# A two-layer hybrid attention block on one core: the later modulation sums move to VectorE, and the first projections are cut in two around three gate blocks

## The chip, the cores and the metric

The kernel runs on one core of a Trainium2 chip. The metric is device time in microseconds (us), the median of several runs of one launch. All inputs and outputs are fp32 in device memory. The engines that matter here are TensorE (PE, matmuls and transposes), VectorE (DVE), ScalarE (ACT), GpSimd (POOL) and the sync engine (SP), from whose queue nearly all transfers are issued. Each engine runs its own instructions in the order in which they were written down.

## The reference, cut to what matters

Two layers over 512 latent tokens and 256 context tokens of width 2048. In each layer a conditioning vector is multiplied by a matrix of 2048 x 6144 and gives shift, scale and gate; this is the modulation. The normalised input times scale plus shift goes through one input projection that feeds three groups of attention heads (A: neighbourhood, B: sliding window, C: latent attention with compressed q and kv) and a gate path z; the heads' outputs times silu(z) go through an output projection, and the result times gate is added to the input.

```
for l in range(DEPTH):                      # DEPTH = 2
    shift, scale, gate       = split(silu(c)     @ w_ada[l] + b_ada[l], 3)
    shift_c, scale_c, gate_c = split(silu(c_ctx) @ w_ada[l] + b_ada[l], 3)
    h  = rms(x,  norm_w[l]) * (1 + scale)   + shift      # 512 latent tokens
    hc = rms(xc, norm_w[l]) * (1 + scale_c) + shift_c    # 256 context tokens
    u  = h @ w_in[l]          # q, k, v of A and B; compressed q and kv, key of C; z
    y  = concat(o_a, o_b, o_c) * silu(z)
    x  = x + gate * (y @ w_out[l])
    # layer 0 does the same for xc; layer 1 needs only k and v of the context
```

There are two vectors, c for the latent tokens and c_ctx for the context, so each modulation block has two sides. In layer 1 only the latent side of the gate is used.

## The kernel before, in words

**Layout.** Tokens are six tiles of 128 (four latent, two context). The modulated input is held transposed, as 16 k-tiles of 128 features by 768 tokens, each split into a high and a low part (hT), and every weight is split likewise ("wh" and "wl", lines 234 and 228 by the helpers sub and act): a product is the sum of three reduced-precision matmuls, high by high, high by low and low by high. A TJob (line 419) is a projection whose output has tokens on the partitions: for each piece of two k-tiles it issues 36 matmuls of 256 columns over three banks of accumulators. An FJob (line 514) makes a block of 128 gate features: four pieces of four k-tiles, in two banks of 384 tokens each. A Group (line 492) takes the pieces of several jobs in turn.

**Planner.** The program is written by a planner, class Weaver: strands of work (fibers) with priorities run against a virtual clock, with a cost for each instruction (lines 210 to 290) and for each transfer (start, line 289: a queue step of 0.475 us, then bytes at 3.6e5 a microsecond). A strand may issue an instruction only when its engine's planned backlog is below AHEAD = 1.35 us. So the order on every engine, SP's queue among them, follows from planned times and priorities; on the chip only semaphores decide when an instruction starts. The list of jobs (main) has priority 6, the lowest; two attention workers and the weight splitter have 2, what comes behind a projection has 1.

**Buffers.** 52 buffers "s3" of 128x768 hold x, hT, heads, and the first modulation weights; "wa" has four buffers of 128x512 for the later ones; "ws" three for weights as loaded. PSUM has six banks "g" and a pair "S", which serves the attention scores and, in the first projections, two of q's banks.

**Modulation.** ada_blocks (line 687) goes through blocks of columns of w_ada. A load is 256 KB, 128 rows by 512 columns (or two k-tiles by 256). Up to depth loads are ahead; a group of them is then multiplied on PE at line 722, with the conditioning vector as 32 columns of weights and the loaded tile streaming through. The four k-tiles of a group stand in different rows of 32 of one bank. ada_finish (line 731) copies the bank, and at line 739 a matmul against the constant "sel" transposes it and adds the four rows. The bias is added, and events tell make_hk that a k-tile's shift and scale are there.

**Order.** Layer 0's shift and scale run at the start in blocks of 256 columns, alternating, with ten loads ahead in groups of two; each pair of blocks releases two k-tiles of hT. The first job is a Group of kv and q of the first two heads of A, piece by piece, as k-tiles are released. Then gate block 0, then the other heads of A and B with gate blocks 1 to 9 among them. Layer 0's gate is started as a strand of priority 4 behind B. Then come C's compressed projections, the rotary key (kpe) and gate blocks 10 to 15, which are stored to device memory; after them hT is freed. Then C's heads, with layer 1's shift and scale beside them in layer 0, and layer 1's gate in layer 1. Last is the output projection, whose last rounds (post_out) multiply by the gate.

post_chunk (line 869) is what follows a kv or q job: per bank, ScalarE copies it out ("raw"), squares and sums follow, then norms, rotary, transposes and the split into heads.

## Time and profile before

| | |
|---|---|
| median of 3 runs | 2972.59 us (2969.92 to 2973.67) |
| the profiled execution | 2976.81 us, of which the span of instructions is 2975.0 |
| granted TensorE clock, mean | 0.994 |
| bytes moved | 349.23 MB, 117 GB/s over the span |
| the first 32 us | PE busy 1.27, the DMA engines full (share 1.02) |
| 32 to 57 us | PE busy 23.00 of 25.00, DMA share 1.02 |
| matmuls on "wa" | from 922.6 to 2692.5 us |

How to read it: a busy share is of the whole span, and one average covers stages with different limits. Busy time of PE counts overlapping matmuls once but holds their pipeline's tail, so that a full row need not mean a full stream. PEld is the loading of PE's weights, which overlaps the matmuls. fp32 matmuls leave two records each in the trace, so that one modulation matmul counts twice. A line such as L234 is that of a helper, and the tile names beside it tell which step it serves. Windows give busy time per engine in the order PE, PEld, DVE, ACT, POOL, then the granted clock, the mean share of the 16 DMA engines, and GB/s.

### The profile page before, as it was taken

The page shows a single profiled execution, that of the slowest core. Times are in us where ns is not written, and L with a number is a line of the kernel's source. Part 1 is how long each engine was busy: PE and PEld are TensorE (multiplying, and loading weights), DVE is VectorE, ACT ScalarE, POOL GpSimd, SP SyncE. Part 2 cuts the span into 40 slices and gives each one's busy share as a digit, 9 for nine tenths or more (in the row PEclk, how much of TensorE's full clock was granted, in tenths as well). Part 3 has the DMA queues.
Part 4 walks back from the last instruction along what each step waited for, and adds up shares of the span by engine and source line. Part 5 has one row for each costly group of instructions (what it writes and reads, how often), then busy time and mean ns, then how long its engine had stood idle before and what let it go on. Part 6 is the DMA issues. An engine that isn't in the chain of part 4 may idle for free.

```text
span 2975.0 us, 56930 instructions
## 1 busy us (share of the span) xinstructions
PE 2882.8 (97%) x21819; PEld 2706.2 (91%) x21819; DVE 1758.5 (59%) x4820; ACT 1254.2 (42%) x2730; POOL 140.1 (5%) x189
## 2 busy tenths in 40 slices
PE   5999999999999999999999999999999999999998
PEld 3689999999999899878999989999998999788998
DVE  5345554637757473867634374655677676578643
ACT  4234333425545452545422273443445455346421
POOL 3000000000100010000000000000000000000000
PEclk9999999999999999999999999999999999999999
DMA  9842222221224555547334333333322214543244
GB/s 253 281 136 81 72 78 76 65 70 49 63 60 127 171 145 157 193 150 237 111 111 124 111 104 82 93 96 91 86 73 66 77 59 129 178 156 118 87 154 127
DMA packets 423633, 349.23 MB, mean 117 GB/s; under 512 B 66276, under 2 KB 370210, under 8 KB 423360
## 3 DMA queue, kind: packets, MB, share of 16 engines
q1 hardware_dynamic: 421488, 344.27, 38.7%
q0 software_dynamic: 1872, 1.32, 0.4%
q8 instruction: 171, 2.80, 0.4%
q14 instruction: 102, 0.84, 0.1%
HBM read 303.97 MB, written 32.08 MB: 113 GB/s over the span
## 4 chain that ended last, share of the span: by engine, by line
PE 88%; DVE 5%; DMA 4%; SPq 1%; ACT 1%; issue 1%; DVEq 0%; ACTq 0%
PE g L323 71%; PE S L323 7%; PE g L326 6%; PE g L722 3%; SPq L293 1%; DMA s<-w_ada 1%; DMA s<-scr 1%; ACT s L228 1%; DVE wl L234 1%; DVE s L234 1%; DVE s L267 1%; DVE pt L234 1%; PE g L739 1%; DVE tm L234 0%; DVE s L256 0%
## 5 line engine op out<-in xcount | busy, mean ns | idle before, releaser
L323 PE MATMUL g<-wh,s 128*128 128x256 f32 (+1 forms) x9000 | 1761.5, 289 | 17.1 <-DVE s L234 7.5
L323 PEld LDWEIGHTS g<-wh,s 128*128 128x128 f32 x9000 | 1445.8, 192 | 54.2 <-issue 31.5
L323 PE MATMUL g<-wl,s 128*128 128x256 f32 (+1 forms) x4500 | 1284.5, 285 | 3.0 <-DVE wl L234 3.0
L323 PEld LDWEIGHTS g<-wl,s 128*128 128x128 f32 x4500 | 862.9, 192 | 5.3 <-DVE wl L234 3.9
L234 DVE TENSOR_TENSOR wl<-ws,wh 128x512 fp32r<-128x512 f32 (+1 forms) x598 | 409.7, 686 | 566.2 <-PE g L323 445.9
L228 ACT ACTIVATE wh<-ws 128x512 fp32r<-128x512 f32 (+2 forms) x606 | 372.0, 615 | 471.8 <-PE g L323 428.2
L323 PE MATMUL g<-s,wh 128*128 128x384 f32 (+1 forms) x1664 | 465.2, 356 | 0.9 <-ACT tm L228 0.9
L228 ACT ACTIVATE s<-s,sm 128x640 f32<-128x640 f32 (+3 forms) x260 | 195.8, 753 | 379.9 <-DVE sm L267 295.4
L323 PEld LDWEIGHTS g<-s,wh 128*128 128x128 f32 x1664 | 304.4, 188 | 21.1 <-ACT tm L228 1.1
L323 PE MATMUL g<-s,wl 128*128 128x384 f32 (+1 forms) x768 | 271.7, 354 | 0.0
L228 ACT ACTIVATE tm<-g 128x512 f32<-128x512 f32 (+4 forms) x324 | 160.7, 517 | 247.6 <-PE g L323 147.5
L234 DVE TENSOR_TENSOR pt<-g,pt 128x512 fp32r<-128x512 f32 (+1 forms) x338 | 196.4, 591 | 92.3 <-ACT pt L228 91.1
L323 PE MATMUL S<-s,s 128*128 128x256 f32 (+2 forms) x1260 | 238.8, 318 | 6.5 <-DVE sm L267 6.1
L326 PE MATMUL g<-ident,s 128*128 128x128 f32 x1520 | 232.7, 277 | 9.8 <-DVE s L234 6.1
L228 ACT ACTIVATE pt<-g 128x512 fp32r<-128x512 f32 (+1 forms) x338 | 168.7, 516 | 155.6 <-PE g L326 149.9
L323 PE MATMUL g<-pt,s 128*128 128x256 f32 (+1 forms) x1348 | 216.7, 286 | 7.4 <-DVE pt L234 4.8
L323 PEld LDWEIGHTS S<-s,s 128*128 128x128 f32 x1260 | 187.2, 190 | 28.6 <-DVE sm L267 12.1
L326 PEld LDWEIGHTS g<-ident,s 128*128 128x128 f32 x1520 | 177.3, 142 | 36.1 <-issue 12.6
L323 PEld LDWEIGHTS g<-pt,s 128*128 128x128 f32 x1348 | 186.5, 192 | 17.6 <-DVE pt L234 7.2
L277 POOL TENSOR_TENSOR s<-ot,s 64x256 f32<-64x256 f32 x100 | 79.3, 794 | 1922.2 <-DVE ot L234 1905.9
L323 PEld LDWEIGHTS g<-s,wl 128*128 128x128 f32 x768 | 144.7, 188 | 9.7 <-DVE wl L234 0.2
L251 DVE TENSOR_SCALAR s<-s,sm 128x640 f32<-128x640 f32 (+3 forms) x260 | 131.8, 507 | 6.1
(146 smaller groups left out, 2129.9 us busy)
## 6 DMA issues: line engine op xcount, KB each, us to landing
wa<-w_ada SPq DMA_DIRECT2D x256, 256.0 KB
ws<-w_in SPq DMA_DIRECT2D x328, 128.0 KB
ws<-w_in SPq DMA_DIRECT2D x160, 256.0 KB
ws<-w_out SPq DMA_DIRECT2D x136, 256.0 KB
s<-w_ada SPq DMA_DIRECT2D x128, 256.0 KB
s<-scr SPq DMA_DIRECT2D x36, 384.0 KB
ws<-w_in SPq DMA_DIRECT2D x64, 192.0 KB
ws<-w_qb SPq DMA_DIRECT2D x54, 192.0 KB
```

The costliest lines, as they stand in the source:

```text
L228: self.nc.scalar.activation(out, in_, func, bias=bias, scale=scale, **kw)
L234: self.nc.vector.tensor_tensor(out, a, b, op=op)
L251: self.nc.vector.tensor_scalar(out, a, s1, s2, op0=op0, op1=op1)
L267: self.nc.vector.tensor_tensor_reduce(out, a, b, -1.0, init, OP.add, OP.min, acc)
L277: self.nc.gpsimd.tensor_tensor(out, a, b, op=OP.mult)
L293: self.nc.sync.dma_start(out, in_)
L323: self.nc.tensor.matmul(out, l, r, start=start, stop=stop, skip_group_check=True)
L326: self.nc.tensor.transpose(out, in_, self.ident)
L722: nc.tensor.matmul(ps[j:j + 32, :n], scT[:, kk, :], s[:, x * n:(x + 1) * n], start=kk < 4, stop=kk >= 12, skip_group_check=True)
L739: nc.tensor.matmul(pt[:, 2 * c:2 * c + 2], a[:, c * 128:(c + 1) * 128], sel, start=c == 0, stop=c == m - 1, skip_group_check=True)
```

## The change

It has four parts.

1. **Later modulation on VectorE.** Layer 0's gate and all of layer 1's modulation no longer pass through PE at line 722. A strand ada_rest, of priority 5, starts once layer 0's shift and scale are done and goes through gate 0, shift and scale 1, gate 1. For each block of 512 columns and each k-tile, VectorE multiplies the loaded tile by the conditioning vector's 128 values for that k-tile (a scalar for each partition) and adds it to an accumulator "ac", one for each side; the strand then pauses for PACE = 4.0 us of planned time. At the block's end, PE adds up the 128 partitions with matmuls of each 128 columns against a column of ones. "wa" and "ac" have two buffers each in place of four "wa". Layer 1's gate is made for the latent side alone.
2. **First projections in two halves.** kv and q of the first two heads become two jobs each, of eight k-tiles. The first halves' banks are copied to "s3" by ScalarE (keep_part); three gate blocks, 10, 11 and 12, follow as a Group, one of them in "S"; then the second halves, to which VectorE adds the copies.
3. **First bursts.** Layer 0's shift and scale run with twelve loads ahead in groups of four (ten and two before).
4. **Planner's costs.** A transfer is planned at 3.1e5 bytes a microsecond, and the matmuls behind a modulation block at 0.21 us (0.05 before).

```diff
-RES = dict(wa=0, s3=8)
+HALF = 8
+RES = dict(s3=8)
+PACE = 4.0
...
-        w.clk["dma"] = max(w.clk["dma"], q + 0.65) + b / 3.6e5
+        w.clk["dma"] = max(w.clk["dma"], q + 0.65) + b / 3.1e5
...
+    def ada_vec(l, c0s, sides):
+        n = 512
+        items = [(c0, k) for c0 in c0s for k in range(KT)]
+        pend = deque()
+        nxt = 0
+        for c0 in c0s:
+            acc = []
+            for k in range(KT):
+                while nxt < len(items) and (not pend or K.free("wa")):
+                    w.cur.ft = w.vt
+                    s = yield from K.get("wa")
+                    c_, k_ = items[nxt]
+                    nxt += 1
+                    ts = yield from K.load_ahead(s, t["w_ada"][l, k_ * 128:(k_ + 1) * 128, c_:c_ + n])
+                    pend.append((s, ts))
+                s, ts = pend.popleft()
+                yield from K.wait(ev_c)
+                w.cur.ft = max(w.vt, ts)
+                if k == 0:
+                    for _ in sides:
+                        acc.append((yield from K.get("ac")))
+                for a, m in zip(acc, sides):
+                    sc = scT[:, k, m:m + 1]
+                    if k == 0:
+                        yield from K.ts(a, s, sc, OP.mult, fast=True)
+                    else:
+                        yield from K.stt(a, s, sc, a, OP.mult, OP.add)
+                K.put("wa", s)
+                yield w.vt + PACE
+            pt = yield from K.get("g")
+            yield from K.sync()
+            for c in range(n // 128):
+                for a, m in zip(acc, sides):
+                    nc.tensor.matmul(pt[:, 2 * c + m:2 * c + m + 1], a[:, c * 128:(c + 1) * 128], one,
+                                     start=c == 0 and m == sides[0], stop=c == n // 128 - 1 and m == sides[-1],
+                                     skip_group_check=True)
+            w.pe(0.21 * n // 128 * len(sides))
+            K.put("ac", *acc)
+            w.spawn(ada_use(l, c0, n, pt, sides), 1, w.cur.ft)
...
+                if part is not None:
+                    yield from K.wait(part[b][1])
+                    yield from K.add(raw, ps[b], part[b][0][:, :512])
+                    K.put("s3", part[b][0])
+                    K.put("g", ps[b])
+                    pv = rv
+                elif direct:
...
+        def keep_part(part):
+            def gen(ps, done):
+                for b in range(len(ps)):
+                    yield from K.wait(done[b])
+                    part[b][0] = yield from K.get("s3")
+                    yield from K.act(part[b][0][:, :512], ps[b])
+                    K.put("g", ps[b])
+                    K.set(part[b][1])
+            return gen
...
+            return [TJob(K, W, runs, cut, tiles, lhs_h, ev_h, keep_part(part)),
+                    TJob(K, W, runs, KT - cut, tiles, lhs_h, ev_h, post, room_chunk(G, blocks), k0=cut)]
...
+            if cut:
+                zs = [zjob(f) for f in (10, 11, 12)]
+                q[0].inS = zs[2].inS = True
+                jobs.extend([Group([kv[0], q[0]]), Group(zs), Group([kv[1], q[1]]), zjob(p)])
...
-        if l == 0:
-            J(lambda: w.spawn(ada_gate(0, "wa", "g", 4, 4), 4))
...
-        for f in range(10, KT):
+        for f in range(10 if last else 13, KT):
...
-        J(lambda: w.spawn(ada_scale(1, 512, "wa", "g", 4, 4) if l == 0 else ada_gate(1, "wa", "g", 4, 4), 4))
...
-    w.spawn(ada_scale(0, 256, "s3", "g", 10, 2), 3)
+    def modulation():
+        yield from ada_scale(0, 256, "s3", "g", 12, 4)
+        w.spawn(ada_rest(), 5)
+
+    def ada_rest():
+        yield from ada_gate(0)
+        yield from ada_vec(1, [c + o for c in range(0, D, 512) for o in (0, D)], (0, 1))
+        yield from ada_gate(1)
+
+    w.spawn(modulation(), 3)
```

More of the change, by code (lines that the diff above doesn't have):

```diff
@@ L544, in step @@
             if p == 0:
-                self.ps[i] = yield from K.get("g")
+                if self.inS:
+                    if i == 0:
+                        pair = yield from K.halves()
+                    self.ps[i] = pair[i]
+                else:
+                    self.ps[i] = yield from K.get("g")
             K.w.cur.ft = tp
@@ L747, in ada_finish @@
         K.put("g", pt)
-        K.put("tm", a)
         k0 = f % KT
@@ L762, in ada_scale, with ada_gate @@
         yield from ada_blocks(l, [(c + o, n) for c in range(0, D, n) for o in (0, D)], stag, ptag, depth, group)
-    def ada_gate(l, stag, ptag, depth, group):
-        yield from ada_blocks(l, [(2 * D + c, 512) for c in range(0, D, 512)], stag, ptag, depth, group)
+    def ada_gate(l):
+        sides = (0, 1) if l == 0 else (0,)
+        yield from ada_vec(l, [2 * D + c for c in range(0, D, 512)], sides)
         yield from K.wait(*ev_gb[l])
@@ L768, in ada_gate @@
         yield from K.sync()
-        for m in range(2):
+        for m in sides:
             K.tr(ps[:KT, m * 128:(m + 1) * 128], ada[l][:, 32:48, m])
@@ L1412, in chunk @@
                     runs.append((c0, 64))
+            part = None if cut is None else [[None, Event()] for _ in range(0, len(tiles), 2)]
             def post(ps, done):
```

56 lines of the change are left out of this document (33 added, 23 removed).

## The prediction

> **What bounds the kernel now.** I read the page's busy times and the chain that ended last, then the table of stretches, then single stretches by line and by time.
>
> ```profile
> span 2975.0 us, 56930 instructions
> PE 2882.8 (97%) x21819; PEld 2706.2 (91%) x21819; DVE 1758.5 (59%) x4820; ACT 1254.2 (42%) x2730; POOL 140.1 (5%) x189
> PE 88%; DVE 5%; DMA 4%; SPq 1%; ACT 1%; issue 1%; DVEq 0%; ACTq 0%
> PE g L323 71%; PE S L323 7%; PE g L326 6%; PE g L722 3%; SPq L293 1%; DMA s<-w_ada 1%; DMA s<-scr 1%; ACT s L228 1%; DVE wl L234 1%; DVE s L234 1%; DVE s L267 1%; DVE pt L234 1%; PE g L739 1%; DVE tm L234 0%; DVE s L256 0%
> ```
>
> The last line holds further entries: TensorE (PE) makes 88% of the chain and is busy for 97% of the span. L722 stands in that chain with 3%: it multiplies the modulation weights. The profiled execution took 2976.81 us (span 2975.0); the three timed runs have their median at 2972.59, 4.2 lower. I make the sum against 2976.8 and take 4.2 off at its end.
>
> ```profile
> 57.00:180.00 123.00, 113.99 (x997) 83.18 (x994) 40.10 (x99) 32.44 (x62) 0.00 (x0) 0.97 0.79 247
> 180.00:980.00 800.00, 794.89 (x6144) 781.44 (x6144) 488.64 (x1437) 348.94 (x810) 51.43 (x63) 1.00 0.28 76
> 980.00:1280.00 300.00, 295.67 (x1998) 266.94 (x1995) 174.99 (x528) 132.41 (x303) 14.60 (x23) 1.00 0.54 169
> ```
>
> The columns are the stretch, its length, and the busy time of PE, PEld, DVE, ACT and POOL. From 180 us to 1280 us PE is idle for only 5.1 + 4.3 = 9.4 us, so an instruction taken from PE there shortens the run by its issue time, as long as nothing else comes late. VectorE (DVE) is busy for 61% of 180 to 980: that is the room the change wants to use.
>
> **Part 1: modulation off PE.** The later modulation (layer 0's gate, all of layer 1's) is 256 loads into "wa".
>
> ```profile
> L722 PE MATMUL g<-wa,scT 128*32 128x512 f32 x512 | 75.8, 609 | 0.5 <-DVE s L256 0.4
> L739 PE MATMUL g<-sel,tm 128*128 128x2 f32 x192 | 23.7, 239 | 0.0
> ```
>
> Its matmuls are 64 groups of four, two records to a matmul. 75.8 us is the upper bound of what goes, since busy spans of pipelined matmuls overlap. For the price in the stream I read one group by time:
>
> ```profile
> 921.82 0.89 PE L323 MATMUL g<-pt,s 128*128 128x256 f32 x6
> 922.64 1.06 PE L722 MATMUL g<-wa,scT 128*32 128x512 f32 x8
> 923.63 0.51 PE L323 MATMUL S<-s,s 128*128 128x256 f32 x2
> 174.78 1.07 PE L722 MATMUL g<-s,scT 128*32 128x256 f32 x16
> 175.78 0.39 PE L323 MATMUL S<-wh,s 128*128 128x256 f32 x1
> 177.31 0.50 PE L739 MATMUL g<-sel,tm 128*128 128x2 f32 x4
> 177.68 0.36 PE L323 MATMUL g<-wh,s 128*128 128x256 f32 x1
> 102.94 2.88 PE S L323 x24
> ```
>
> The last row is from the chain: 24 matmuls of 256 columns in 2.88 us, 0.12 each. The six "pt" matmuls from 921.82 should therefore be over at 922.54, and the next work after the group begins at 923.63: 1.09 us a group, 64 x 1.09 = 70 us. From its own start to the next it is 0.99, 63 us, the lower bound. I take **-69**.
>
> What PE gets back: with the sum over k on VectorE, each 128 columns of an accumulator still need a matmul against a column of ones to bring the 128 partitions together. Layer 0's gate and layer 1's scale and shift have 12 blocks x 4 x 2 sides = 96, layer 1's gate 4 x 4 x 1 = 16, so 112. In place of them 16 blocks x 4 = 64 matmuls against "sel" go. The rows at 177.31 and 177.68: two such matmuls (four records) push the next one by 0.37 to 0.5 us, about 0.21 each. (112 - 64) x 0.21 = **+10** us. A one-column output is not in the trace; the two-column one is next to it, bounds +5 to +15.
>
> **Part 2: what VectorE gets.** 28 block accumulators (12 x 2 + 4) start with a tensor_scalar, and the other 15 of 16 steps are scalar_tensor_tensor with a scalar from SBUF: 28 + 420 instructions of 128x512.
>
> ```profile
> L256 DVE SCALAR_TENSOR_TENSOR s<-s,qaT,s x12: 740/886/1019, 1104.4 to 2561.2; 128x768 fp32r<-128x768 f32 x6, 128x512 fp32r<-128x512 f32 x6
> L251 DVE TENSOR_SCALAR s<-s,sm 128x512 f32<-128x512 f32 x80 | 39.3, 491 | 1.6
> L234 DVE TENSOR_TENSOR wl<-ws,wh 128x512 fp32r<-128x512 f32 (+1 forms) x598 | 409.7, 686 | 566.2 <-PE g L323 445.9
> DVE wl L234 <- PE g L323: 445.9, 209, 5.4
> ```
>
> The qaT rows are the same operation on two fp32 SBUF tiles with a scalar from SBUF: 128x512 at the minimum, 740 ns. So 420 x 0.74 + 28 x 0.49 = 325 us more on VectorE, 1.48 a step for two sides and 0.74 for one. The loop yields 4.0 us after each step and its loads and gates add a little; at 4.2 us its 256 steps run from about 180 to 1255. In 180 to 980 it would add 800 / 4.2 x 1.48 = 282 us to 488.6: 771 of 800, 96% busy.
>
> The Trainium skill (Vector Engine (DVE) Microarchitecture Reference, "7. Points that are easy to get wrong") speaks against this: it says that a scalar_tensor_tensor with two SBUF sources that aren't bf16 runs at half throughput. The trace disagrees: 740 to 1019 ns over 256 more elements is 1.09 ns an element, about the same as for any single-rate row. By the rule each would take some 0.56 us more; the measured row decides, and the rule is kept below as a rival.
>
> Does PE wait for VectorE at 96%? Queued behind each new instruction on VectorE's in-order queue are the weight splits ("wl"), which PE needs for every projection, the row maxima of the softmax, and the subtractions behind transposes. Cover: the splits waited 445.9 us in all, longest 5.4, for PE to free a buffer, so they stand ready some 4 us ahead. I took VectorE's busy time in the 60 stretches of 20 us from 180 to 1380, added the new work, and carried over what didn't fit. The first, the last and those that overflow most:
>
> ```profile
> 180.00:200.00 20.00, 19.15 (x133) 18.92 (x134) 12.92 (x38) 9.68 (x23) 0.00 (x0) 1.00 0.35 93
> 720.00:740.00 20.00, 19.07 (x157) 18.63 (x156) 16.79 (x45) 9.25 (x22) 3.29 (x3) 1.00 0.20 60
> 740.00:760.00 20.00, 18.65 (x149) 17.64 (x148) 14.05 (x46) 12.35 (x34) 2.89 (x4) 1.00 0.20 51
> 760.00:780.00 20.00, 19.58 (x131) 19.26 (x130) 16.89 (x58) 9.85 (x29) 1.48 (x2) 1.00 0.15 40
> 920.00:940.00 20.00, 19.40 (x159) 16.44 (x157) 18.74 (x62) 8.07 (x21) 4.22 (x5) 1.00 0.45 145
> 1360.00:1380.00 20.00, 19.09 (x141) 15.80 (x134) 13.97 (x33) 12.74 (x26) 0.00 (x0) 1.00 0.67 222
> ```
>
> With no slack the overflow sums to 41 us at a 4.2 us step (46 at 4.0); with 4 us of slack PE loses 16. The other reading is by likeness: 720 to 780, where VectorE is 80% busy, has PE idle for 2.7 of 60 us, and 4.5% over 1100 us, less the 9.4 there now, would be +40. But at 920 to 940 VectorE is at 94% and PE loses 0.6 of 20, 3%, +24. I take **+18**, between the slack estimate and the last one; bounds 0 and +46. The lower end is not below nothing, since nothing that VectorE did goes away except small adds.
>
> A step also waits for its own "wa" load, two buffers in place of four; a late one would hold all of VectorE. The loads are issued a step (4 us) ahead and the 16 DMA engines are at about 0.28 there, so I cost this at nothing; without that cover, 0.3 us on one step in eight is 10 us, within the bounds. On SP's queue the same 256 loads stand earlier among the weight loads, from about 180 on in place of 922, no more of them. POOL's queue is untouched. ScalarE loses 16 copies. The edit that saves matmuls is thus worth -69 + 10 + 18 = -41.
>
> **Part 3: the start.** Up to 57 us PE waits for x, and nothing here changes that but a first group of four loads in place of two. From 57 to 180:
>
> ```profile
> L323 PE MATMUL g<-wh,s 128*128 128x256 f32 x226 | 49.0, 300 | 2.3 <-DVE s L234 1.9 <-ACT s L228 0.4
> L722 PE MATMUL g<-s,scT 128*32 128x256 f32 x428 | 40.9, 401 | 6.0 <-DMA s<-w_ada 5.1
> L323 PE MATMUL g<-wl,s 128*128 128x256 f32 x113 | 32.3, 286 | 0.0
> L323 PE MATMUL S<-wh,s 128*128 128x256 f32 x112 | 22.4, 289 | 0.0
> L323 PE MATMUL S<-wl,s 128*128 128x256 f32 x56 | 15.8, 282 | 0.0
> ```
>
> 226 + 113 + 112 + 56 = 507 matmuls x 0.12 = 61 us; 428 modulation records at 1.0 us for 16 (175.78 - 174.78 above) = 27; about 7 for "sel" and transposes. That is 95 of 123 us: 28 us are loss, mostly waits for the modulation loads, though the row says busy.
>
> ```profile
> PEld g L722 <- DMA s<-w_ada: 14.4, 23, 2.3
> PE g L722 <- DMA s<-w_ada: 5.1, 5, 1.9
> ```
>
> Before, kv and q for the last pair of k-tiles must wait for the last modulation block: 7/8 of their 576 x 0.12 = 69 us can go ahead, 60. After, the first half (34.5) and three quarters of three gate blocks can. A gate block is 96 matmuls of 384 columns:
>
> ```profile
> 1099.95 0.51 PE L323 MATMUL g<-s,wh 128*128 128x384 f32 x2
> 1100.47 0.51 PE L323 MATMUL g<-s,wh 128*128 128x384 f32 x2
> ```
>
> Three in 0.52, so 16.6 us a block, 37 for three quarters: 72 us against 60, 12 more to fill waits with. Against it: the weights needed ahead of the last block are 2 + 2.3 MB in place of 3.5, at about 250 GB/s +3 us of a stretch that the loads limit. The six partial copies (ScalarE) and six adds (VectorE, 0.69 each by the "wl" row) run where VectorE is a third busy (40.1 of 123): nothing. The second halves take all six "g" banks, so the next gate block waits for the first add, +2 if nothing covers it. Deeper loading (12 for 10, groups of four) saves some group switches, up to 4. Sum **-9**, bounds -28 and +8. The three gate blocks leave the stretch before layer 0's latent attention (1100 to 1160), where they only filled; what they hid (the last parts of the compressed q, which come in once the gate blocks free their inputs) is late already, and I put +0 on it, at most +5: the waits on "wa" loads leave the same stretches.
>
> ```profile
> 1120.00:1140.00 20.00, 20.00 (x118) 20.00 (x117) 4.52 (x7) 3.92 (x7) 0.00 (x0) 1.00 0.30 84
> 1160.00:1180.00 20.00, 18.40 (x102) 14.73 (x100) 9.68 (x17) 10.04 (x20) 0.00 (x0) 1.00 0.81 263
> PEld g L722 <- DMA wa<-w_ada: 5.5, 11, 1.0
> ```
>
> PE is full at 1120 with little on the others, loses 1.6 us at 1160 now, and 5.5 to late "wa" loads in all.
>
> **The sum.** -69 + 10 + 18 - 9 = -50: 2976.8 - 50 = 2926.8, less 4.2: **2923**.
>
> **Rivals.**
> (a) VectorE becomes the bound: slower. PE then idles between 180 and 1280 because the planner lays VectorE's work too densely. It decides when PE's idle time there grows by more than 69 - 10 + 9 = 68 us, from 9.4 to 77, 7% of 1100. At twice the share of 720 to 780 (9%), it is 99 - 9 = +90, in all +22: 2995. For it: 96% on average with stretches over 100%. Against: PE's small loss at 94%, and other matmuls to turn to. 8 in 100.
> (b) The whole overflow lands on PE and the start gains nothing: -69 + 10 + 46 = -13: 2960. 17 in 100 for this and its neighbourhood (2945 to 2966); about the same time (2967 to 2978) another 5.
> (c) Half-rate scalar_tensor_tensor: 420 x 0.56 = 235 us more on VectorE, of which about 210 don't fit into 180 to 980: 2923 + 190 = 3113. The qaT row speaks against it. 1 in 100.
> (d) The change doesn't do what it says: the background loop falls behind and layer 1 waits for its modulation. Its 192 steps must be over when layer 1's norm is taken:
> ```profile
> L256 DVE SCALAR_TENSOR_TENSOR rx<-sm,rx x12: 152/161/164, 34.6 to 1748.0; 128x4 f32<-128x4 f32 x6, 128x2 f32<-128x2 f32 x6
> ```
> At 1748 that allows 8 us a step. Should it need 9, layer 1 starts 160 us late: 3083. 1 in 100.
> (e) Better than the sum: VectorE costs nothing and the start gains 20: -79, 2893. 15 in 100. The forecast itself (2900 to 2945): 53.
>
> **How the numbers follow.** Faster by over 0.2% (6 us, about what a measurement can tell): 53 + 15 + 17 = 85. Within: 5. Slower: 8 + 1 + 1 = 10. The range takes in the forecast, (b), half of the cases of about the same time and most of (e), 2886 to 2972; outside are the 10 of slower and some 5 of the other cases at its ends.
>
> **What would show it.** Right: L722 left with 512 records, all on "s"; VectorE near 2080 us in all and scalar_tensor_tensor on "ac" near 0.74; PE busy about 60 less; PE idle between 180 and 1280 near 27; modulation matmuls of the start over by 180. Wrong: PE idle there over 77, or "ac" instructions near 1.3 us; a start that ends later than now; waits of PE for DVE "wl" as the longest entry.

## The result, and the profile after

The changed kernel takes 2952.32 us (median of four runs, 2948.53 to 2956.37), the kernel before 2973.13 in the same comparison (2969.92 to 2978.33): a ratio of 0.9929, with a 95% interval of 0.9907 to 0.9950. It is faster by 21 us. The prediction was 2923, 50 us faster; the sign is right, the gain is well under half of the forecast. The profiled execution took 2949.59 us, near the fast end of the four, so the traces differ by a little more (27 us) than the medians.

From the page of the changed kernel: the span, the busy times, and the chain by engine and by line.

```profile
span 2947.8 us, 56481 instructions
PE 2826.9 (96%) x21402; PEld 2715.2 (92%) x21402; DVE 2025.8 (69%) x5275; ACT 1243.7 (42%) x2714; POOL 144.8 (5%) x189
PE 81%; DVE 11%; DMA 4%; issue 2%; SPq 1%; ACT 1%; DVEq 0%; ACTq 0%
PE g L327 67%; PE S L327 6%; PE g L330 5%; DVE wl L238 2%; DMA s<-w_ada 2%; SPq L297 1%; DVE s L271 1%; DVE s L238 1%; DVE ac L260 1%; DVE pt L238 1%; PE g L792 1%; DVE tm L238 1%; DVE s L260 1%; DVE s L255 1%; ACT s L232 1%
```

PE is busy for 55.9 us less (2882.8 to 2826.9), close to the 60 that were forecast. But the span fell by only 27.2, so PE is idle for 28.7 us more: the forecast had 18 - 9 = 9 more. In the chain PE went from 88% to 81% and VectorE from 5% to 11%, with the new instruction (DVE ac L260) in it. All lines have moved by four or more: L323 is now L327, L722 is L734, L234 is L238, L256 is L260.

Where the idle time is, by windows of the changed kernel (stretch, length, busy PE, PEld, DVE, ACT, POOL, granted clock, DMA share, GB/s):

```profile
57.00:180.00 123.00, 115.18 (x970) 90.58 (x970) 38.78 (x91) 33.93 (x65) 0.00 (x0) 1.00 0.81 249
180.00:980.00 800.00, 781.12 (x5921) 768.91 (x5920) 618.68 (x1565) 313.34 (x715) 46.63 (x52) 0.99 0.40 114
980.00:1280.00 300.00, 280.93 (x2016) 273.28 (x2015) 265.52 (x758) 151.36 (x359) 28.00 (x34) 0.98 0.41 121
800.00:900.00 100.00, 90.09 (x577) 86.32 (x576) 87.08 (x249) 48.18 (x127) 9.22 (x12) 0.91 0.33 95
1150.00:1440.00 290.00, 265.60 (x1828) 252.44 (x1827) 259.96 (x723) 154.04 (x351) 12.99 (x22) 0.97 0.44 135
```

The same windows of before, and 700 to 800, where its window heads stand:

```profile
700.00:800.00 100.00, 96.91 (x718) 94.13 (x717) 80.21 (x253) 54.06 (x140) 11.08 (x13) 1.00 0.22 61
800.00:900.00 100.00, 100.00 (x781) 100.00 (x781) 60.69 (x178) 44.02 (x107) 7.19 (x9) 1.00 0.21 55
1150.00:1440.00 290.00, 280.84 (x1965) 236.63 (x1964) 214.37 (x626) 150.66 (x340) 4.34 (x7) 0.99 0.59 195
```

From 180 to 1280 PE is idle for 38 us; it was 9.4, and 27 were forecast. The extra idle time is not spread out. Two stretches hold most of it, both with VectorE at 87% or more: 9.9 us in 800 to 900 (the window heads of B; before has 3.1 in 700 to 800, where the same heads stand some 50 us earlier), and 24.4 in 1150 to 1440 (the projections and attention of C's heads), where the same window of before gives 9.2. In both the granted clock falls too.

The last record of "rx", the norm that opens layer 1, splits the run by layers; first the changed kernel:

```profile
L260 DVE SCALAR_TENSOR_TENSOR rx<-sm,rx x12: 154/161/164, 35.5 to 1749.0; 128x4 f32<-128x4 f32 x6, 128x2 f32<-128x2 f32 x6
```

It is at 1749.0, against 1748.0 before. Layer 0, which lost three quarters of the modulation groups, gained nothing at all. The whole gain came in layer 1, where layer 1's gate was taken from PE and VectorE had nothing new to do any more (its last accumulation starts at 1634.0): after that norm 1198.8 us are left, before 1227.0.

### The profile page after: what moved, and what is told of

Its sections match the earlier page's. It is cut to its first block, busy times and chain, and to the rows that moved or that the text cites. A ratio compares the mean times of both kernels' runs of the same rounds, so it can differ in the third digit from the quotient of the medians.

```text
span 2947.8 us, 56481 instructions
## 1 busy us (share of the span) xinstructions
PE 2826.9 (96%) x21402; PEld 2715.2 (92%) x21402; DVE 2025.8 (69%) x5275; ACT 1243.7 (42%) x2714; POOL 144.8 (5%) x189
## 4 chain that ended last, share of the span: by engine, by line
PE 81%; DVE 11%; DMA 4%; issue 2%; SPq 1%; ACT 1%; DVEq 0%; ACTq 0%
PE g L327 67%; PE S L327 6%; PE g L330 5%; DVE wl L238 2%; DMA s<-w_ada 2%; SPq L297 1%; DVE s L271 1%; DVE s L238 1%; DVE ac L260 1%; DVE pt L238 1%; PE g L792 1%; DVE tm L238 1%; DVE s L260 1%; DVE s L255 1%; ACT s L232 1%
## 5 line engine op out<-in xcount | busy, mean ns | idle before, releaser
L327 PE MATMUL g<-wh,s 128*128 128x256 f32 (+1 forms) x9064 | 1766.7, 288 | 18.7 <-DVE tm L238 6.5
L327 PEld LDWEIGHTS g<-wh,s 128*128 128x128 f32 x9064 | 1457.7, 192 | 28.9 <-issue 9.1
L327 PE MATMUL g<-wl,s 128*128 128x256 f32 (+1 forms) x4532 | 1295.7, 286 | 6.5 <-DVE wl L238 6.3
L327 PEld LDWEIGHTS g<-wl,s 128*128 128x128 f32 x4532 | 870.7, 192 | 10.8 <-DVE wl L238 9.5
L238 DVE TENSOR_TENSOR wl<-ws,wh 128x512 fp32r<-128x512 f32 (+1 forms) x598 | 410.6, 687 | 455.6 <-PE g L327 262.7
L327 PE MATMUL g<-s,wh 128*128 128x384 f32 (+1 forms) x1600 | 453.4, 358 | 1.1 <-DVE s L238 0.6
L260 DVE SCALAR_TENSOR_TENSOR ac<-wa,scT,ac 128x512 f32<-128x512 f32 x420 | 311.7, 760 | 9.2 <-DMA wa<-w_ada 8.3
L327 PEld LDWEIGHTS g<-s,wh 128*128 128x128 f32 x1600 | 294.3, 189 | 25.0 <-issue 2.1
L327 PE MATMUL g<-s,wl 128*128 128x384 f32 (+1 forms) x736 | 261.7, 356 | 0.0
L330 PE MATMUL g<-ident,s 128*128 128x128 f32 x1520 | 234.3, 279 | 20.1 <-DVE s L255 10.3
L327 PE MATMUL S<-s,s 128*128 128x256 f32 (+2 forms) x1260 | 240.6, 320 | 12.1 <-DVE sm L271 11.2
L232 ACT ACTIVATE tm<-g 128x512 f32<-128x512 f32 (+4 forms) x298 | 146.6, 513 | 226.3 <-PE g L327 126.8
L238 DVE TENSOR_TENSOR pt<-g,pt 128x512 fp32r<-128x512 f32 (+1 forms) x338 | 196.8, 591 | 65.0 <-ACT pt L232 63.8
L327 PE MATMUL g<-pt,s 128*128 128x256 f32 (+1 forms) x1348 | 223.0, 289 | 12.7 <-DVE pt L238 7.9
L327 PEld LDWEIGHTS S<-s,s 128*128 128x128 f32 x1260 | 188.9, 191 | 27.1 <-DVE sm L271 17.9
L330 PEld LDWEIGHTS g<-ident,s 128*128 128x128 f32 x1520 | 179.7, 143 | 33.0 <-DVE s L255 13.7
L327 PEld LDWEIGHTS g<-pt,s 128*128 128x128 f32 x1348 | 188.8, 193 | 22.1 <-DVE pt L238 12.8
L281 POOL TENSOR_TENSOR s<-ot,s 64x256 f32<-64x256 f32 x100 | 87.3, 873 | 1976.9 <-DVE ot L238 1943.1
L327 PEld LDWEIGHTS g<-s,wl 128*128 128x128 f32 x736 | 139.3, 189 | 9.4
```

Of the source, the lines that this page charges most:

```text
L232: self.nc.scalar.activation(out, in_, func, bias=bias, scale=scale, **kw)
L238: self.nc.vector.tensor_tensor(out, a, b, op=op)
L260: self.nc.vector.scalar_tensor_tensor(out, a, s, b, op0=op0, op1=op1)
L281: self.nc.gpsimd.tensor_tensor(out, a, b, op=OP.mult)
L327: self.nc.tensor.matmul(out, l, r, start=start, stop=stop, skip_group_check=True)
L330: self.nc.tensor.transpose(out, in_, self.ident)
```

## The experiments

Two questions: is it the loop on VectorE that holds up PE, and if so by what? The theory (T1) is that the loop's instructions stand in VectorE's queue in front of what PE waits for, in the stretches where VectorE is nearly full. The rivals: the new start and the moved gate blocks cost it (T2 in the first four runs); the modulation matmuls on PE had only filled waits, so that taking them away could not give 70 us (T2 from hold_c on); the loop's own loads hold VectorE up; the planner's two new cost figures spoil the order. Every kernel was timed beside the kernel before on the same chip; "norm" is the last "rx" record of its trace, "rest" the span after it.

| kernel | median us | before | ratio, 95% | norm | rest |
|---|---|---|---|---|---|
| before | | | | 1748.0 | 1227.0 |
| changed | 2952.32 | 2973.13 | 0.9929, 0.9907 to 0.9950 | 1749.0 | 1198.8 |
| vec_only | 2948.36 | 2976.74 | 0.9904, 0.9891 to 0.9918 | 1745.1 | 1197.5 |
| start_only | 2970.25 | 2976.74 | 0.9976, 0.9967 to 0.9985 | 1745.3 | 1223.5 |
| pace7 | 2984.24 | 2976.74 | 1.0027, 1.0016 to 1.0039 | 1728.2 | 1254.4 |
| half_vec | 2933.95 | 2976.74 | 0.9860, 0.9846 to 0.9873 | 1732.0 | 1199.5 |
| hold_c | 2941.13 | 2972.05 | 0.9887, 0.9873 to 0.9901 | 1739.5 | 1199.5 |
| pace55 | 2944.15 | 2972.05 | 0.9899, 0.9884 to 0.9914 | 1736.0 | 1205.0 |
| gates_vec | 2964.02 | 2972.05 | 0.9967, 0.9954 to 0.9979 | 1756.3 | 1200.7 |
| narrow_mm | 2954.22 | 2972.05 | 0.9934, 0.9921 to 0.9948 | 1733.2 | 1221.8 |
| loop_only | 3002.10 | 2974.06 | 1.0089, 1.0075 to 1.0104 | 1771.0 | 1229.5 |
| cut_groups | 2915.86 | 2974.06 | 0.9801, 0.9787 to 0.9815 | 1701.1 | 1210.8 |
| hold_bc | 2926.50 | 2974.06 | 0.9841, 0.9821 to 0.9861 | 1721.4 | 1202.6 |
| hold_bc_old | 2937.91 | 2974.06 | 0.9875, 0.9860 to 0.9891 | 1735.7 | 1204.4 |
| cut_plus_loop | 2939.73 | 2976.80 | 0.9874, 0.9859 to 0.9889 | 1726.7 | 1212.2 |
| no_loads | 2944.51 | 2976.80 | 0.9891, 0.9873 to 0.9908 | 1743.1 | 1198.2 |
| cost_only | 2975.77 | 2973.28 | 1.0005, 0.9996 to 1.0014 | 1753.3 | 1223.5 |
| vec_oldcost | 2958.30 | 2973.28 | 0.9951, 0.9939 to 0.9964 | 1757.3 | 1199.2 |
| after_oldcost | 2947.97 | 2973.28 | 0.9913, 0.9897 to 0.9928 | 1745.1 | 1202.8 |
| hold_oldcost | 2930.05 | 2973.28 | 0.9853, 0.9835 to 0.9871 | 1721.8 | 1205.9 |

### The two halves of the change: vec_only and start_only

vec_only keeps the new modulation and puts the start and the gate blocks back:

```
-            cut = HALF if not last and p == 0 else None
+            cut = None
...
-        for f in range(10 if last else 13, KT):
+        for f in range(10, KT):
...
-        yield from ada_scale(0, 256, "s3", "g", 12, 4)
+        yield from ada_scale(0, 256, "s3", "g", 10, 2)
```

> The changed kernel, but with the start of before: kv and q in one piece, gate blocks 10 to 12 back ahead of layer 0's latent attention, ten loads ahead in groups of two. Before is 2973, the change 2952. Theory 1 (VectorE's loop makes TensorE wait, about 45 us of the 59 that leave it, and the start is worth nothing): 2948 to 2957, with TensorE idle for about 30 us between 180 and 1440 us as after the change. Theory 2 (the new start and the moved gate blocks cost some 20 us, the loop itself is nearly free): 2925 to 2937.

start_only is the other half: new start, bursts and planner figures, with all modulation on PE as before.

```
-        w.spawn(ada_rest(), 5)
+        J(lambda: w.spawn(ada_gate(0), 4))
...
+        J(lambda: w.spawn(ada_scale(1, 512, "wa", "g", 4, 4) if l == 0 else ada_gate(1), 4))
```

> The new start, bursts and planner's costs alone; the later modulation stays on TensorE as before. Before is 2973. Theory 1 (the loop on VectorE is what cost): between 2966 and 2975, the start worth little either way. Theory 2 (the start and the moved gate blocks cost): 2985 to 3000, with TensorE idle ahead of layer 0's latent attention. The prediction's own term was -9: 2964.

The modulation alone gives 28 us, the start alone 6.5. Neither is the culprit by itself, and most of the loss sits in the modulation: 28 us where -69 + 10 + 18 = -41 had been forecast. The two halves would add up to 35; together they gave 21.

### The loop's pace and size: pace7, half_vec, pace55

```
-PACE = 4.0
+PACE = 7.0
```

> The change with a pause of 7.0 us in place of 4.0 after each step of the loop: the same instructions, spread thinner, over by about 2020 us, layer 1's shift and scale by about 1560, ahead of the 1749 at which they are wanted. VectorE's share from 180 to 980 falls from some 90% to near 82%. Theory 1 (VectorE's queue is too dense): 2925 to 2938. Theory 2 (start and gate blocks): 2950 to 2955, as with 4.0.

Slower than before, which neither theory had, and for another reason than a busy VectorE. Layer 0 gained 21 us (norm at 1728.2). Then layer 1 had to wait, since its shift and scale came too late. The last row of "gsc", the finished scale, in pace7:

```profile
L260 DVE SCALAR_TENSOR_TENSOR gsc<-ada,nT x12: 155/163/208, 55.0 to 1795.7; 128x4 f32<-128x4 f32 x8, 128x8 f32<-128x8 f32 x4
```

It is finished at 1795.7, after the norm, and PE is idle for 44.5 us of 1760 to 2490, against 6.1 in the changed kernel. This is the prediction's rival (d), made real by hand: the loop is late, and layer 1 pays.

half_vec does the context's side in a block's first step only and leaves out its other 15, so that 180 of the 420 accumulations go:

```
-                    else:
+                    elif m == 0:
```

> The change with the context side of the loop left out behind its first step (15 of 16 instructions of that side; its modulation is then only the first k-tile's): the same loads, steps and pause, but half of VectorE's added work in the two-sided blocks. Theory 1: 2928 to 2940. Theory 2: 2948 to 2955. Theory 3 (the steps' waits for their loads hold VectorE, not the arithmetic): no better than 2948 either, since all loads and waits remain.

18 us faster than the changed kernel by medians, of which layer 0 has 17: less VectorE work on the same loads and the same PE work gives time back, as T1 says. The gain lies in the first of the two stretches: PE is idle for 3.6 us in 800 to 900, but still for 23.7 in 1150 to 1440, where the loop, which had run ahead, has 56 instructions against 71 in the changed kernel. pace55 spreads the loop without being late:

```
-PACE = 4.0
+PACE = 5.5
```

> Pause of 5.5 us in place of 4.0: layer 1's shift and scale should be over ahead of layer 1's start at about 1735, which they weren't with 7.0 (1796, where layer 1 waited some 40 us). Theory 1 (density of the loop): layer 0 is over earlier, as it was with 7.0 (layer 1's norm at 1728 in place of 1749), and nothing waits at its end: 2932 to 2943. Theory 2: 2948 to 2956.

Ratio 0.9899, norm at 1736.0: 13 us of layer 0 came back, 6 of them went again in layer 1, where the loop now runs until 2045.9. That is 1 us outside T1's range and nearer to it than to T2's.

### Pausing the loop: hold_c, hold_bc, hold_bc_old

hold_c stops the loop from the point where hT is freed until the projections of C's heads are through; in its trace the loop stands still from 1182 to some 1390, most of 1150 to 1440:

```
+                if hold[0]:
+                    yield lambda: None if hold[0] else 0.0
                 s, ts = pend.popleft()
...
         J(free_h)
+        J(lambda: hold.__setitem__(0, not last))
...
+        J(lambda: hold.__setitem__(0, False))
         J(lambda: need.__setitem__(0, 3))
```

> The change, but the loop on VectorE stands still from the end of layer 0's gate blocks to the end of its latent-attention projections (about 1160 to 1400 us) and goes on after it. Theory 1 (in that stretch the loop's instructions hold up TensorE): TensorE's idle time from 1150 to 1440 falls from 24 us to about 10, as before the change, and the run takes 2935 to 2944. Theory 2 (TensorE's modulation matmuls had only filled waits there, which stay when they go, loop or no loop): idle stays near 20 and the time near 2952.

As T1 had it: ratio 0.9887, some 12 us faster than the changed kernel, and PE's idle time in 1150 to 1440 falls from 24.4 to 12.9 us. In 800 to 900, with the loop as before, it stays at 9.8.

hold_bc pauses it also between B's first kv job and its second q job, and is hold_c otherwise:

```
                 jobs.append(kv_job(GB, "B", g))
+                if g == 0:
+                    J(lambda: hold.__setitem__(0, not last))
...
             jobs.append(q_job(GB, "B", range(3 * g, 3 * g + 3), (8 + g,)))
+            if g == 1:
+                J(lambda: hold.__setitem__(0, False))
```

> As hold_c, and the loop also stands still while layer 0's first q projections of the window heads are made (about 760 to 880 us), where the change left TensorE idle for 10 us and its clock at 0.91. Layer 1's shift and scale are then over near 1620, ahead of 1735. Theory 1: idle from 800 to 900 falls to about 3 and its clock to above 0.97; 2925 to 2934. Theory 2: as hold_c, 2938 to 2943.

Windows of hold_bc:

```profile
700.00:800.00 100.00, 99.53 (x788) 99.08 (x787) 77.48 (x228) 46.44 (x111) 8.00 (x9) 1.00 0.24 63
800.00:900.00 100.00, 96.09 (x700) 93.51 (x699) 89.10 (x251) 49.49 (x128) 9.13 (x11) 1.00 0.37 103
1150.00:1440.00 290.00, 277.16 (x1969) 266.52 (x1968) 243.59 (x685) 161.30 (x362) 10.69 (x20) 0.98 0.35 105
```

PE's idle time falls from 9.9 to 3.9 us in 800 to 900, with the clock back at 1.00, and from 24.4 to 12.8 in 1150 to 1440. Layer 0 is 27.6 us shorter than in the changed kernel (norm 1721.4), the loop still ends in time, and at 2926.5 it is the fastest version that still computes everything: 48 us faster than before, about 26 faster than the change. The work and the bytes are the same. 17.6 us of the 27.6 are idle time of PE in those two stretches, and the clock of the first one, back from 0.91, is worth up to 9 more. So most of the change's missing gain lay there, and it hung on how the loop is placed.

The first pause did not fall where it was meant to. On the chip the loop stands still from 695 to 765, ahead of the stretch. In 800 to 900 it has 36 instructions, where the changed kernel has 32, and VectorE is as full (89.10 and 87.08). So neither VectorE's share nor the loop's density in a window of 100 us decides by itself. That the order within VectorE's queue does is the reading that is left; no run tests it alone.

> As hold_bc, with the start of before (projections in one piece, gate blocks 10 to 12 late, ten loads in groups of two). If the new start is worth the few us that it showed alone (2970 of 2977): 3 to 8 slower than hold_bc. If it is worth nothing beside the loop (the loop with the old start took 2948, the change 2952): equal within 4 or faster.

That is hold_bc with the old start of vec_only. It is 11 us slower than hold_bc, more than the 3 to 8 expected: beside the pauses the new start is worth about what was forecast (9). Against vec_only, which has the same start, the pauses gave only 9 us (0.9875 for 0.9904).

### Doing less on PE: gates_vec, narrow_mm

gates_vec leaves layer 1's shift and scale on PE and moves the gates only; the accumulators are taken from the "s3" buffers:

```
-        yield from ada_vec(1, [c + o for c in range(0, D, 512) for o in (0, D)], (0, 1))
...
+            J(lambda: w.spawn(ada_scale(1, 512, "wa", "g", 4, 4), 4))
```

> Only the two layers' gates on VectorE (accumulators in the large buffers, over by about 850 us); layer 1's shift and scale stay on TensorE beside the latent attention, as before. Theory 2 (what stood on TensorE beside the latent attention was free filler, so only the gates' 32 groups and not the other 32 were worth moving): as fast as the change or faster, 2936 to 2950. Theory 1 (every group moved gains its 1.09 us and loses to VectorE in proportion): half the gain, 2960 to 2966.

Only 8 us. Layer 1 kept its gain (rest 1200.7), layer 0 lost 8 (1756.3). PE was idle for some 15 us in 200 to 800 (before 3.7), 6.2 of it before transposes that wait for VectorE's L255. Because the accumulators took other buffers, this is not a clean half of the change, and I draw nothing more from it.

narrow_mm is the kernel before with 12 of 16 later modulation matmuls 16 columns wide in place of 512 (most columns of their sums are left out):

```
+                    wd = n if stag == "s3" or kk < 4 else 16
-                    nc.tensor.matmul(ps[j:j + 32, :n], scT[:, kk, :], s[:, x * n:(x + 1) * n],
+                    nc.tensor.matmul(ps[j:j + 32, :wd], scT[:, kk, :], s[:, x * n:x * n + wd],
```

> The kernel before with the same order of instructions, but 12 of every 16 later modulation matmuls made 16 columns wide in place of 512 (their sums are left out; loads, waits and order stay, nothing is added on VectorE). 48 of 64 groups get shorter by some 0.85 us, 41 in all: 10 in layer 0's gate, 20 in layer 1's shift and scale, 10 in layer 1's gate. Theory 1 (all of it was on the path): 2930 to 2937, layer 1's norm near 1718 in place of 1748. Theory 2 (the part beside layer 0's latent attention was filler): the 20 there come back as idle TensorE: 2950 to 2956, layer 1's norm at 1735 or later.

18 us for 48 groups made some 0.85 us shorter each (41 us): less than half. PE's idle time in 1150 to 1440 went from 9.2 to 17.3 us without any new work on VectorE, so that part of the matmul time there had only filled waits. That spoke for the fill theory, and the next pair tested it.

### The two prices by themselves: cut_groups, loop_only, cut_plus_loop

cut_groups is the kernel before with 4 of the 16 k-tiles of the later modulation: 48 of 64 groups go with their loads.

```
-        items = [(c0, n, k) for c0, n in blocks for k in range(0, KT, 512 // n)]
+        items = [(c0, n, k) for c0, n in blocks for k in range(0, KT if stag == "s3" else 4, 512 // n)]
...
```

> The kernel before with only the first 4 of 16 k-tiles of the later modulation (the other 12 are left out, with their loads): 48 of 64 groups leave TensorE, their waits and loads too, and nothing is added. It prices TensorE's part alone. The prediction's price of 1.09 us a group: -52, 2920. If the groups beside the latent attention had half filled waits (as the narrow matmuls had it): 2935 to 2945.

58.2 / 48 = 1.21 us a group, its loads included. Whole groups were not fill: taking them away gives more than the 1.09 of the forecast, and that rival falls. In narrow_mm the groups with their loads and weights stayed, which may be why they kept their waits.

loop_only is the kernel before with the loop's accumulations on a resident tile, 448 of them with a pause of 5.3 us in place of 4.0; nothing is loaded and nothing leaves PE, and the result is not used.

```
+        for i in range(256):
+            w.cur.ft = w.vt
+            for m in ((0, 1) if i < 192 else (0,)):
+                yield from K.stt(a, f, scT[:, i % KT, m:m + 1], f, OP.mult, OP.add)
+            yield w.vt + 5.3
```

> The kernel before, with the loop's VectorE instructions added and nothing taken from TensorE: 448 scalar_tensor_tensor of 128x512 on a resident tile, 192 steps of two and 64 of one, a step about every 5.6 us from 180 on, no loads, results unused. It prices VectorE's part alone. Before is 2972. Theory 1 (VectorE's queue holds up TensorE; needed to close the account: about 30): 2992 to 3010, with TensorE idle and a lower granted clock where the neighbouring head groups meet (750 to 850) and beside the latent attention. Theory 2 (the loop itself is nearly free, the loss lies in what TensorE's matmuls had filled): 2970 to 2980.

28 us slower: the loop alone costs more than the 18 that were forecast, although it is thinner than the change's (339 of its instructions between 190 and 1300, where the change has 382). Windows of loop_only:

```profile
700.00:800.00 100.00, 90.16 (x632) 86.84 (x632) 90.09 (x260) 46.75 (x121) 11.00 (x13) 0.93 0.15 41
1150.00:1440.00 290.00, 280.47 (x1920) 235.64 (x1919) 247.73 (x675) 143.70 (x328) 1.60 (x3) 1.00 0.59 193
```

Again the window heads (in the old order of gate blocks they come some 50 us earlier, at 700 to 800): 9.8 us idle where before had 3.1, and the clock down to 0.93. In 1150 to 1440 there is no loss (9.5 idle, 9.2 before).

cut_plus_loop is both edits together.

> The kernel before with 48 of the 64 groups of later-modulation matmuls and their loads left out (as in cut_groups, 58 us faster), and with the loop of VectorE instructions on a resident tile added (as in loop_only, 28 us slower). Its modulation is therefore not the reference's and the loop's result is not used. Theory that the two add up: -58 + 28 = -30, about 2944. Theory that the loop costs more where TensorE has lost its modulation matmuls: -58 + 45 to 50 = -13 to -8, 2961 to 2966.

-37, where -58 and +28 make -30. They add up or come out a little better; beside the cut the loop costs 21. That the loop becomes dearer once PE has lost its own modulation is refuted for the three quarters of it that were cut. Its windows:

```profile
57.00:200.00 143.00, 136.08 (x1150) 104.57 (x1147) 60.08 (x147) 41.90 (x84) 0.00 (x0) 1.00 0.74 229
1150.00:1440.00 290.00, 279.74 (x1995) 261.95 (x1994) 258.66 (x721) 158.53 (x360) 4.50 (x7) 0.98 0.37 117
```

VectorE is as full in 1150 to 1440 as in the changed kernel (258.7 and 260.0), but PE is idle for 10.3 us and not for 24.4.

### What else the loop brings: no_loads, and the planner's figures

no_loads is the changed kernel with a resident tile in place of the weights, and a pause of 4.6 us, meant to keep its steps as long:

```
-                while nxt < len(items) and (not pend or K.free("wa")):
+                while False:
...
-                s, ts = pend.popleft()
+                s = scT.rearrange("p k n -> p (k n)")
...
-PACE = 4.0
+PACE = 4.6
```

> The changed kernel whose loop multiplies a resident tile in place of the weights it would load: the 256 loads into wa are left out, so layer 0's gate and layer 1's modulation are not the reference's; the pause after a step is 4.6 us in place of 4.0, so that a step lasts as long as before. Theory that the loop's loads hold up VectorE's queue: the waits of ac on the DMA (17 us in the trace) and what stands behind them go, and it is 15 to 25 us faster than the changed kernel, 2927 to 2937. Rival, that the loads cost nothing on the path and the loop's own instructions make all the delay: 2948 to 2955.

Between the two: 2944.5, by the ratios 11 us better than the changed kernel, and the intervals (0.9873 to 0.9908, 0.9907 to 0.9950) just touch. The steps came out longer, though: the last "gsc" record, behind the 192nd step, is at 1421.2 and not at 1304.1, so part of the 11 us may come from the thinner loop, as in pace55. The price of the loads is therefore not measured by itself; up to some 11 us fit. They do hold VectorE up; in the changed kernel's waits by tile "wa":

```profile
  DVE ac L253: 9.0, 2
  DVE ac L260: 8.3, 7
```

17 us in nine waits, and the whole of VectorE stands still in them.

The last four runs tried the two planner figures that the change also alters, since vec_only and start_only share a worse start (PE idle for 13.7 and 11.3 us in 57 to 200, before 9.9). cost_only makes that edit alone in the kernel before:

```
-        w.clk["dma"] = max(w.clk["dma"], q + 0.65) + b / 3.6e5
+        w.clk["dma"] = max(w.clk["dma"], q + 0.65) + b / 3.1e5
...
-        w.pe(0.05 * m)
+        w.pe(0.21 * m)
```

> The kernel before with only the planner's two figures of the change (0.21 for 0.05 us a sel matmul, 3.1e5 for 3.6e5 bytes per us). Theory that these figures spoil the order: 5 to 15 us slower, 2980 to 2990. Rival, that they do nothing: within 3 us.

The other three undo that edit in vec_only, in the changed kernel and in hold_bc:

> The change of the modulation alone (old start, as vec_only, ratio 0.990) with the planner's two figures as before. Theory that the figures spoil the order: 8 to 18 us faster than vec_only, ratio 0.984 to 0.988. Rival: ratio 0.990 again.

> The whole change, but for the planner's two figures, which stay as before. Theory that the figures spoil the order: 8 to 18 us faster than the changed kernel, ratio 0.987 to 0.990. Rival, that they do nothing: ratio 0.993 again; that they are needed for the new start: slower than that.

> hold_bc (ratio 0.984) with the planner's two figures as before. If the figures cost the start some 8 us whatever the loop does: ratio 0.981. Rival, no effect: 0.984.

The theory fell: alone the figures do nothing (1.0005). Undoing them made vec_only slower (0.9951 for 0.9904), the changed kernel perhaps faster (0.9913 for 0.9929, within the intervals), and hold_bc the same (0.9853 for 0.9841). What they show is another thing: a small edit of the planner reorders the program, and with the loop in it the same work then comes out up to 14 us apart. Two of the three prices of the pauses are larger than that: 26 us with the new figures, 18 with the old ones (0.9853 for 0.9913); the 9 beside the old start is not.

## Why the prediction was right and wrong

**The step that failed is "Does PE wait for VectorE at 96%?", the term of +18.** It took the slack of the weight splits for the slack of everything that PE needs from VectorE. Three things in it were off.

First the density. The loop's step was taken as 4.2 us; on the chip it is 5.8. The "gsc" record of the 192nd step is at 1304.1 and the loop began at 190: 1114 / 192. With pauses of 5.5 and 7.0 us the steps are 7.5 and 8.4 us (pace55, pace7): the step's own instructions, 1.48 us and more, come on top of the pause. VectorE is therefore at 618.7 of 800 us and not at 771, and rival (a), which needed that density, was further off than it looked. By the prediction's own reckoning this should have made the term smaller; it came out larger.

Second, and worse, the cover. The slack was read from the weight splits ("wl"), which stand some 4 us ahead. They still do, mostly: PE's waits for them are 6.3 us in all. But other waits of PE for VectorE are longer and grew more. Before and in the changed kernel (engine and line, what it waited for, total us, times, longest):

```profile
PE S L323 <- DVE sm L267: 6.1, 12, 1.3
PE g L326 <- DVE s L251: 0.9, 3, 0.5
PE g L323 <- DVE pt L234: 4.8, 9, 1.5
PE g L323 <- DVE wl L234: 3.0, 4, 1.7
...
PE S L327 <- DVE sm L271: 11.2, 16, 2.4
PE g L330 <- DVE s L255: 10.3, 14, 2.0
PE g L327 <- DVE pt L238: 9.7, 17, 1.3
PE g L327 <- DVE wl L238: 6.3, 10, 2.3
```

The first three of each are the softmax maxima, the scaled probabilities and the low parts of their transposes: links of a chain that passes back and forth between PE and VectorE. They grew from 11.8 to 31.2 us, 19.4 of the 28.7 by which PE is idle for longer; the splits grew by 3.3. The prediction had named them as queued behind the new instruction, and then took the slack of the splits for all of them. One link, first on VectorE and then on PE, from the two timelines of the changed kernel (start, length):

```profile
811.46 0.69 DVE L238 TENSOR_TENSOR wl<-ws,wh 128x512 fp32r<-128x512 f32 x1
812.07 0.75 DVE L260 SCALAR_TENSOR_TENSOR ac<-wa,scT,ac 128x512 f32<-128x512 f32 x1
812.73 0.68 DVE L238 TENSOR_TENSOR pt<-g,pt 128x512 fp32r<-128x512 f32 x1
...
819.14 0.48 DVE L253 TENSOR_SCALAR ac<-wa,scT 128x512 f32<-128x512 f32 x1 [2.00 <-PE g L792]
```

```profile
809.85 1.03 PE L330 MATMUL g<-ident,s 128*128 128x128 f32 x8
812.30 0.39 PE L327 MATMUL g<-pt,s 128*128 128x256 f32 x1 [1.42 <-ACT pt L232]
813.47 0.62 PE L327 MATMUL g<-pt,s 128*128 128x256 f32 x3 [0.78 <-DVE pt L238]
...
816.01 3.51 PE L792 MATMUL g<-one,ac 128*128 128x1 f32 x16
...
826.43 0.90 PE L330 MATMUL g<-ident,s 128*128 128x128 f32 x3 [1.83 <-DVE s L255]
```

The accumulation of 812.07 stands in front of "pt"; without it "pt" would begin 0.66 us earlier, and PE waits 0.78 for it. Then VectorE in its turn waits 2.00 us for PE to be through with the column sums of an accumulator.

Third, that a wait costs only itself: the clock, below.

So the size was not 18. The loop alone measured +28, beside the cut +21, both with a thinner loop than the change's, and what its loads add is up to some 11 more. The two readings by likeness, +24 and +40, which I had set aside for the slack estimate, came nearer. The loads of the loop, put at nothing, are part of the same miss; how large a part isn't known.

**The other terms.** The price of a group, 1.09, measured 1.21 with its loads and waits: 64 x 1.21 = 78 rather than 69. The one-column matmuls were right: eight of them (16 records) hold up the next matmul by 1.71 us in the changed kernel's timeline, 0.21 each.

```profile
267.22 1.84 PE L792 MATMUL g<-one,ac 128*128 128x1 f32 x16
268.93 0.36 PE L327 MATMUL g<-wh,s 128*128 128x256 f32 x1
```

Four pairs of runs differ in the start alone, and by their ratios it gives -9 (start_only against cost_only), -10 (hold_bc against hold_bc_old), -11 (after_oldcost against vec_oldcost) and +7 (the changed kernel against vec_only). So -9 holds in three orders of the program, and not in the changed kernel itself. There the first matmul of the A heads' position bias ("flip") comes at 265.1, 51 us later than before (214.0), and three gate blocks at 16.6 us are 50: the stretch ahead of it gained nothing. The moved gate blocks, put at "+0, at most +5", leave PE idle for 6.2 us of 1150 to 1210 in the changed kernel and for 4.0 in start_only, against 1.6 before: the upper end of that term.

**What stays open.** The parts by themselves make -78 + 10 (column sums) + 21 to 28 (loop) - 6.5 (start and planner figures) + up to 11 (loads) = -54 to -36, and 21 were measured. So 15 us or more are not accounted for by single parts. By layers the gap is wider: layer 1 gained 28 us for 16 groups, where cut_groups gained 16 there for 12, so layer 0, which gained nothing, hides more. The trace shows where most of it lies: compared with cut_plus_loop, which has the loop without loads, column sums and the new start, and still a quarter of the groups on PE, the changed kernel's PE is idle for 5.5 us more in 57 to 200 and 14.1 more in 1150 to 1440. Of the 5.5, some 3 are scatter between executions: hold_bc, the same program up to 695, is idle for 9.3 there, the changed kernel for 12.4. The pauses bring most of the 14.1 back. Why a VectorE equally full costs that much more there isn't settled. It isn't the loads (no_loads is idle for 27.3 us there), and hardly the column sums (4.6 us of PE in that stretch); with the gate blocks at their old place it was 17.0 us in vec_only, but 24.3 in vec_oldcost. The groups that PE no longer has, and the mere order, are left, and the scatter of up to 14 us between orders is as large as what is open.

**The rivals and signs.** (a) had its turning point at 68 us of added idle time between 180 and 1280, and 28.5 came. (b), the overflow on PE and no gain at the start, 2960, is nearest by its number. Its mechanism was not at work as it was told: over 180 to 980 VectorE had 181 us to spare, and PE waited for single links of a chain, not for work that did not fit. That the time came out near (b) is in part luck. Of the signs of a wrong forecast one came: the start's last modulation matmul begins at 184.0 (175.5 before), not by 180. Waits for "wl" as the longest entry did not come, since the waits were elsewhere. (c) is refuted: the prediction weighed the Trainium skill (Vector Engine (DVE) Microarchitecture Reference, "7. Points that are easy to get wrong"), by which such an instruction runs at half throughput, against the qaT row, and the new instructions themselves show the full rate.

```profile
L260 DVE SCALAR_TENSOR_TENSOR ac<-wa,scT,ac x420: 730/746/1509, 189.6 to 1634.0; 128x512 f32<-128x512 f32 x140
```

Their median is 746 ns, as forecast. VectorE's 2025.8 instead of 2080 has the same work in it, 311.7 + 13.6 = 325 us of new instructions; one that stands in the queue starts before the last is over (812.07 and 812.73 above, 0.66 apart at 0.75 each), and busy time counts that once (the times of VectorE's groups add up to 339 us more than before, its busy time to 267 more). (d) did not come about here, but pace7 shows that a longer pause would have led to it. (e), 2893, was not reached by any version.

## What to carry to other kernels

When work moves to an engine with room, its free share over a stage says little: look for the consumer with the least slack behind that engine's queue (here the softmax chain, not the weight splits with 4 us in hand), and price the move by the stretches where that chain runs. Try pauses of a background loop around those stretches, and check its deadline at the far end: two pauses gave 9, 18 and 26 us in three orders of this program, though one of them did not stand where it was meant to, so look for it in the trace. Slowing the loop everywhere by 1.5 us a pause gave 9 us, by 3 us it made the kernel slower than before. Test both prices by themselves, the work taken out and the work put in, and expect that mere reordering scatters the rest by some 10 us, as it did in this dense program.

## What the runs showed of the hardware

Behind a cluster of short waits of PE the granted clock is lower. In the changed kernel:

```profile
800.00:810.00 10.00, 9.25 (x73) 8.61 (x72) 9.71 (x28) 6.17 (x15) 1.30 (x1) 1.00 0.51 155
810.00:820.00 10.00, 7.53 (x43) 6.74 (x41) 6.77 (x19) 3.47 (x9) 0.71 (x1) 0.77 0.20 60
820.00:830.00 10.00, 7.46 (x34) 6.20 (x33) 7.73 (x27) 4.19 (x13) 0.72 (x1) 0.67 0.17 52
830.00:840.00 10.00, 10.00 (x70) 10.00 (x70) 9.17 (x29) 6.18 (x18) 0.73 (x1) 0.87 0.18 54
840.00:850.00 10.00, 10.00 (x67) 9.96 (x66) 9.73 (x30) 5.04 (x14) 1.70 (x2) 1.00 0.26 79
```

PE is idle for 5.8 us of these 50, and the clock goes to 0.67: the missing clock adds up to (0.23 + 0.33 + 0.13) x 10 = 7 us of full speed. The eight column sums at 816.01 take 3.38 us until the next matmul, twice the 1.71 at full clock. From 800 to 900, 9.9 us of waits are joined by 9% of lost clock, so the waits there may cost nearly twice what they show. The Trainium skill (TensorE: Matmul & The Clock Gate, "Part 1: The HAM clock gate") puts the fall to half clock behind an idle window of about 3.4 us. Here it came without a single wait that long: the longest from 809 to 830 is 1.83, with transposes, column sums and short runs of attention matmuls in between. Which of these matters isn't shown.
